# Four moves in the first head of a hybrid mLSTM and HGRN2 step: gate exponentials, decay exponentials, weight loads, a convolution

## The chip, the core and the metric

The kernel runs on one core of one Trainium2 chip. The metric is the device time of one execution in microseconds (us). Engines are called as the profile calls them: PE is TensorE's matmuls, PEld its weight loads, ACT is ScalarE, DVE is VectorE, POOL is GpSimd, SP is SyncE, which here only issues DMAs. "L1042" is line 1042 of the kernel before.

## The reference, cut to what matters

One inference step of a one-layer streaming encoder. 512 prompt frames of a new stream and 32 frames of a running stream go through it together, so the kernel's row length T is 544. Two branches work on the same normalised input: an mLSTM with 4 heads of width 512 and an HGRN2 with 8 heads of width 128. The change is all within the mLSTM's first head.

```python
xn = _rmsnorm(h, norm_g[l])
proj = xn @ w_in[l]
u, v_m, z_m, ig_pre, fg_pre, q_h, f_h, i_h, g_h, ga, gb = jnp.split(proj, ...)
c, conv_new = _causal_conv(u, conv0[l], conv_w[l], conv_b[l])   # 4 taps
c = jax.nn.silu(c)
qm, km = c @ w_qm, (c @ w_km) * M_HD ** -0.5        # per head
lf = jax.nn.log_sigmoid(fg_pre + b_fg[l])
# _mlstm, per head, chunk by chunk:
dmat = jnp.exp(logd - m_t[..., None])               # decay between positions
s = (q @ k^T) * dmat
num = w_inter * (C @ q) + s @ v                     # C: memory from before
C_new = decay * C + (w_last * v)^T @ k
...
hm = _head_layernorm(hm, mnorm_g[l])
hm = (hm + m_skip[l] * c) * jax.nn.silu(z_m)
ya = hm @ w_brm[l]                                  # mLSTM's branch output
```

The HGRN2 branch (`yb`), the sigmoid merge of `ya` and `yb`, `w_out`, the per-layer embedding and a final norm follow. Everything is float32.

## The kernel before, in words

**Precision.** A float32 product is made of three fp32r products. Each operand is split into a high part, which ACT makes as a rounded copy, and a low part, which DVE makes by subtraction: `split` does it for activations (L105, L106) and `split_piece` for pieces of weights (L132, L133). A name with `h` or `l` at its end is one of these parts, and one with `r` in it is the raw piece that a DMA loaded. A matmul group on low parts cannot start before ACT and then DVE are done.

**Tiling.** Weights come as pieces of 128 rows by 512 columns through a ring of buffers. An output tile has 128 rows and is made as two halves of 272 columns in PSUM. `phalves` gives these from four banks, and `paux` gives one of two double banks to everything else (scores `sc`, transposes `kt`, `kts` and `yt`, the old memory's product `nm`).

**Order.** PE runs one list of matmuls in a fixed order (`tc.manual_schedule` holds PE's order as written). On ACT, DVE, POOL and SP a scheduler sets the order, from the order in which the code issues the instructions, from `tc.high_priority()`, and from `tc.issue_after(x)`, which holds an instruction back in that order until x. Each engine then runs its list strictly in order, so one that waits holds up everything behind it. Between the steps of a head a `Pump` gives PE blocks of projection (`d`, from `fill(h)`: this head's `z`, the next head's `u`, the merge gates), so that PE has work while ACT and DVE make the next operands.

**Head 0, in time order.** (1) The head's values `vp` (L1397) are made from eight weight pieces `wv0` to `wv7`, k = 0 to 7, four banks at a time, with ACT and DVE scaling and splitting the input at the same time (`norm` L1287 and L1290, `norm_low` L1294; the tiles are `x`, `xh`, `xl`). Among them `stage_gates` makes the forget gates' log-sigmoid on a 4-row tile (`row`): an Exp and a Ln (L727, L728), each with a load of ACT's table. `vq` (L1407) is the running stream's value product, `vhl`, `vh` and `vl` are the values out of PSUM (`value_out`, L1317 and L1318), and the first blocks of `d` (L387: `z`, on weights `wi32`) follow on the banks that these release. (2) `stage_k`, `stage_q` make keys and queries; `qf` (L857) and `q` (L860, L861) are the copies of the queries out of PSUM. (3) `stage_decay` loads the row maxima to all partitions (`bc`), and ACT makes the decay tiles `dm` with ten exponentials and one small one (L810, L811). `hgrn_bounds` adds one small exponential (`lbe`). A dummy silu (L866) then loads the silu table. (4) `stage_scores` (L881) multiplies queries by keys, and DVE multiplies by the decay (L889). (5) `mchain`: keys are transposed (`kt`) and weighted (`kwh`, `kwl`), old memory `c` is loaded in four pieces (L986), and `nm` (L1042) multiplies it by the decayed queries `qw`; then new memory (`C`), scores by values (`nm` L1096), the layer norm, and the transposes `yt` (L1144). DVE adds the skip path (L1151, L1152, in `c0` to `c3`), multiplies by `silu(z)` (L1153), and `split` makes `hm0` to `hm3`. (6) `stage_br` multiplies these by `w_brm` (pieces `wbm`) to `ya` (L167), and ACT copies it out (L1171).

The next head's causal convolution is made tile by tile in `conv`: one scaling on ACT (L646), three DVE multiply-adds (L651, `cv`), a silu on ACT (L657, L658), and a split to `cs4` and so on (the names go on over the heads: `cs4` to `cs7` are head 1's). Its first tile is called from `inner` (in `fill`), when the `u` tile is out of PSUM, and the others from `stage_br` after each of its `u` steps.

Of the kernel before, what the change touches and what calls it, by code (L numbers as in the profile page):

```python
# [9 lines left out]
F32 = mybir.dt.float32  # L10
# [3 lines left out]
AF = mybir.ActivationFunctionType  # L14
# [8 lines left out]
T = NS + NP  # L23
# [43 lines left out]
def hybrid_step(ctx: ExitStack, tc: tile.TileContext, a, o):  # L67
# [34 lines left out]

    def split(src, name):
        hi, lo = slot(name + "h", F32R), slot(name + "l", F32R)
        S.copy(hi[:, :T], src)  # L105
        V.tensor_tensor(lo[:, :T], src, hi[:, :T].bitcast(F32), ALU.subtract)  # L106
        return hi, lo

    def pair_tile(name, ring):
# [562 lines left out]
    def fill(h):  # L672


        def value(f, t):
            st8[h]["vt"][f] = t

        def gate(f, t):
            act = S.activation(t[:, :T], t[:, :T], AF.Silu)
            st8[h]["z"][f] = (t, act)  # L680

        def gate_one(f, acc):
            z = eslot(f"z{h}{f}")
            for b in range(2):
                with tc.high_priority():
                    if f < 2:
                        out = V.tensor_tensor(z[:, half(b)], acc[b][:, :TH], rb[:, half(b)], ALU.mult)
                    else:
                        out = V.tensor_copy(z[:, half(b)], acc[b][:, :TH])
            st8[h].setdefault("copies", []).append(out)  # L690
            act = S.activation(z[:, :T], z[:, :T], AF.Silu)
            st8[h]["z"][f] = (z, act)

        def inner_tile(f):
            ub = conv_tile((h + 1) * KH + f)
            return ub, conv_parts(ub)

        def inner(f, ub):
            st8[h + 1]["ub"][f] = ub
            if f == 0:  # L700
                conv(h + 1)

        st8[h]["z"] = [None] * KH
        todo = []
        if h:
            st8[h]["vt"] = [None] * KH
            todo += [pair("v", f, 16 + h * KH + f, lambda f: plain(eslot(f"vt{h}{f}")), value) for f in (0, 2)]
            todo += [pair("z", f, 32 + h * KH + f, lambda f: plain(eslot(f"z{h}{f}")), gate) for f in (0, 2)]
        else:
            todo += [One(("z", f), 32 + f, TH, lambda acc, f=f: gate_one(f, acc), x0 if f < 2 else None) for f in range(KH)]  # L710
        if h + 1 < MH:
            st8[h + 1]["ub"] = [None] * KH
            todo += [pair("u", f, (h + 1) * KH + f, inner_tile, inner) for f in (0, 2)]
            todo[-1].urgent = True
        return todo
# [76 lines left out]
                combo[(b, b + i)] = len(combo)  # L792
        return col, cols, combo

    def stage_decay(h):

        bc = tp.tile([P, T + NS], F32, tag="bc", name=f"bc{h}")
        nc.sync.dma_start(bc, nm_d[h : h + 1, :].to_broadcast([P, T + NS]))
        d01 = [slot(f"dm{h}0"), slot(f"dm{h}1")]
        d2 = slot(f"dm{h}2")  # L800
        dj = [d01[0][:, 0:512], d01[1][:, 0:384], d2[:, 0:256], d2[:, 256:384]]
# [4 lines left out]
        for j in range(NB):  # L806
            for i in range(j, NB):
                d = dj[j][:, (i - j) * P : (i - j + 1) * P]
                src = d if i == j else bc[:, NS + i * P : NS + (i + 1) * P]
                S.activation(d, src, AF.Exp, bias=col[:, combo[(j, i)], h : h + 1])  # L810
# [35 lines left out]
    def stage_q(h, u):  # L846
# [6 lines left out]
        for f in range(2):  # L853
# [6 lines left out]
                    read = S.copy(qh[:, half(b)], acc[b])  # L860
                    low = V.tensor_tensor(ql[:, half(b)], acc[b], qh[:, half(b)].bitcast(F32), ALU.subtract)  # L861
            t["qs"].append((qh, ql))
        if u:

            with tc.issue_after(read.ins):
                S.activation(small("silu", [1, 2]), ident[:1, :2], AF.Silu)  # L866
        return low

    def stage_scores(h):
# [86 lines left out]
    def mchain(h, pump):  # L956
# [26 lines left out]
            low = V.scalar_tensor_tensor(kws[lo], pt[lo, 0, :], wc[lo], kws[lo].bitcast(F32), ALU.mult, ALU.subtract)  # L983
        c0 = [eslot(f"c0{h}{f}") for f in range(KH)]
        for f in range(KH):
            nc.sync.dma_start(c0[f][:, :VW], a["C0"][h, f])  # L986

        if h == 0:
            vv, vs = t["vv"], t["vs"]
# [146 lines left out]
        for f in range(KH):  # L1136
# [13 lines left out]
            with tc.high_priority():  # L1150
                V.scalar_tensor_tensor(c[:, NS:T], pt[:, 0, :], g, c[:, NS:T], ALU.mult, ALU.add)  # L1151
                V.scalar_tensor_tensor(c[:, :NS], pt[:, 1, :NS], g, c[:, :NS], ALU.mult, ALU.add)  # L1152
            V.tensor_tensor(c[:, :T], c[:, :T], z[:, :T], ALU.mult)  # L1153
            hs.append(split(c[:, :T], f"hm{ft}"))
# [62 lines left out]
    with tc.manual_schedule(engines={mybir.EngineType.Activation, mybir.EngineType.DVE, mybir.EngineType.PE}):  # L1217
# [147 lines left out]
        for k in range(KD):  # L1365
            if k == 1:
# [71 lines left out]
    with tc.manual_schedule(engines={mybir.EngineType.PE}):  # L1438
        for h in range(MH):
# [14 lines left out]
            if h == 0:  # L1454
# [561 lines left out]
```

## Time and profile before

| what | value |
|---|---|
| time, median of 3 runs | 1132.48 us (1131.96 to 1132.76) |
| the profiled execution's own time | 1132.39 us |
| its span in the trace | 1130.5 us |
| its granted PE clock, mean | 0.998 |
| PE busy | 1112.0 us, 98% of the span |
| DVE, ACT and POOL busy | 79%, 59% and 15% |
| HBM traffic over the span | 138 GB/s |

The span is the time from the trace's first to its last instruction; 1.9 us of the execution lie around it. PE is idle for some 18 us in all, and that is where the table must be read with care: a busy share of 98% over the whole program says nothing on the stretch in which head 0 runs. Most of PE's waits are there.

### The profile page before, as it was taken

Reading aid. Unit: us, or ns where it says so; the run is one execution under the profiler, and the core shown is the slowest. Engines: PE = TensorE matmul, PEld = TensorE weight load, DVE = VectorE, ACT = ScalarE, POOL = GpSimd, SP = SyncE. Lnnn points to the kernel's source line nnn. Section 1 sums busy time; section 2 is a strip of 40 time slices with the busy share of each in tenths; the row PEclk is TensorE's granted clock in tenths of the full one; section 3 lists DMA queues with packets and bytes.
Section 4 is the critical chain, followed back from the end, with each engine's and each line's share of the span. In section 5 each row is a group of like instructions: output and inputs, shape, how many; then the busy total and the mean of one; then the engine's idle time right before and its main releaser. Section 6 shows DMA issues by size and latency. Waiting matters only on the chain.

```text
span 1130.5 us, 23774 instructions
## 1 busy us (share of the span) xinstructions
PE 1112.0 (98%) x8733; PEld 1087.1 (96%) x8733; DVE 895.3 (79%) x2040; ACT 670.6 (59%) x1506; POOL 169.2 (15%) x308
## 2 busy tenths in 40 slices
PE   9999998999999999999999999999999999999998
PEld 9879898999999999999999999999999999999998
DVE  6888878578697695986888799999999977654485
ACT  6677356655566463765556467776776667333462
POOL 7223000000020000200100122322332210000000
PEclk9999999999999999999999999999999999999999
DMA  6133323513344232553667666666765685332753
GB/s 229 55 112 108 103 85 96 161 54 123 128 154 165 63 115 104 163 167 96 188 188 223 196 140 147 136 144 147 157 140 148 158 220 161 117 102 72 260 152 117
DMA packets 90139, 157.94 MB, mean 140 GB/s; under 512 B 10148, under 2 KB 17828, under 8 KB 90024
## 3 DMA queue, kind: packets, MB, share of 16 engines
q1 hardware_dynamic: 80352, 139.33, 39.0%
q0 software_dynamic: 8784, 15.99, 9.1%
q8 instruction: 68, 1.11, 0.4%
q10 hardware_dynamic: 888, 1.12, 0.3%
q14 instruction: 47, 0.39, 0.1%
HBM read 131.49 MB, written 24.91 MB: 138 GB/s over the span
## 4 chain that ended last, share of the span: by engine, by line
PE 90%; DVE 5%; DMA 2%; ACT 2%; issue 1%; SPq 0%; POOL 0%; ACTq 0%; DVEq 0%
PE d L502 37%; PE ya L167 8%; PE pg L1863 4%; PE yb L167 4%; PE o L167 4%; PE q L167 4%; PE C L921 4%; PE k L167 4%; PE nm L1096 3%; PE sc L881 3%; PE pl L1635 2%; PE u L287 2%; PE vp L1397 1%; PE ple L167 1%; PE d L387 1%
## 5 line engine op out<-in xcount | busy, mean ns | idle before, releaser
L420 POOL DMA_DIRECT2D ws<-in_w_in x46 | 40.4, 884 | 237.6 <-DVE hkq L1659 49.5
L516 ACT COPY t<-d 128x272 f32<-128x272 f32 x126 | 47.7, 378 | 8.8 <-PE d L502 8.7
L1659 DVE TENSOR_TENSOR hkq<-hkq,q 128x288 f32<-128x288 f32 (+1 forms) x96 | 40.7, 430 | 3.3 <-ACT t L516 1.2
L1635 PE MATMUL pl<-hkq,km 128*128 128x128 f32 x224 | 37.8, 291 | 1.2 <-ACT km L1624 1.1
L651 DVE SCALAR_TENSOR_TENSOR cv<-ub,vec,cv 128x547 f32<-128x547 f32 x48 | 37.6, 782 | 0.4
L1635 PEld LDWEIGHTS pl<-hkq,km 128*128 128x128 f32 x224 | 31.2, 189 | 2.7 <-ACT km L1624 2.3
L1624 ACT COPY km<-hkq 128x256 f32<-128x256 f32 x56 | 24.0, 428 | 14.0 <-DVE hkq L1659 4.6
L1030 DVE SCALAR_TENSOR_TENSOR c<-c,wi,Cs 128x258 f32<-128x258 f32 x32 | 15.3, 479 | 18.5 <-PE Cs L1028 18.2
L933 ACT COPY Co<-C 128x258 f32<-128x258 f32 x30 | 9.8, 378 | 30.6 <-PE C L921 28.3
L1174 DVE TENSOR_TENSOR y<-ya,y 128x272 f32<-128x272 f32 x48 | 18.8, 434 | 8.8 <-PE ya L167 8.7
L1666 DVE COPY_PREDICATED at<-lmask,pl 128x256 f32<-128x256 uint8 (+1 forms) x56 | 25.2, 450 | 0.1
L1107 ACT COPY y<-nm 128x516 f32<-128x516 f32 x16 | 9.5, 591 | 22.7 <-PE nm L1096 22.4
L643 POOL COPY uo<-ub 128x3 f32<-128x3 f32 x16 | 17.5, 1092 | 34.9 <-DVE ub L525 27.5
L1603 POOL TENSOR_SCALAR_AFFINE_SELECT aa<-at 128x128 f32<-128x128 f32 x32 | 19.6, 643 | 8.2 <-DVE at L1666 8.0
L821 POOL COPY vsm<-vt 128x96 f32<-128x96 f32 x12 | 7.3, 607 | 87.7 <-DVE vt L523 45.3
L1084 DVE BATCH_NORM_STATS2 bs<-y 128x6 f32<-128x512 f32 (+1 forms) x20 | 13.8, 689 | 8.0 <-ACT y L1107 7.8
L477 POOL DMA_DIRECT2D ws<-in_w_in x15 | 15.6, 1037 | 28.3 <-DVE ws272l L133 23.6
L1096 PE MATMUL nm<-vhl,sh 128*128 128x258 f32 x112 | 18.4, 286 | 0.6 <-ACT y L1107 0.6
L895 ACT CAST sh<-dm 128x512 fp32r<-128x512 f32 (+3 forms) x16 | 7.4, 460 | 17.7 <-DVE dm L889 17.7
L1850 DVE TENSOR_TENSOR h<-o,h 128x272 f32<-128x272 f32 x16 | 6.3, 436 | 14.5 <-PE o L167 14.5
L1765 ACT ACTIVATE osq<-kq 128x128 f32<-128x128 f32 x32 | 9.8, 305 | 12.3 <-DVE kq L1760 12.1
L1837 DVE TENSOR_TENSOR gb<-yb,gb 128x272 f32<-128x272 f32 x16 | 6.3, 435 | 13.1 <-PE yb L167 13.1
(4496 smaller groups left out, 4998.4 us busy)
## 6 DMA issues: line engine op xcount, KB each, us to landing
ws<-in_w_in POOLq DMA_DIRECT2D x61, 256.0 KB, 4.9
ws<-in_w_in SPq DMA_DIRECT2D x46, 256.0 KB, 3.9
ya_d<-y SPq DMA_DIRECT2D x32, 272.0 KB, 2.2
y<-ya_d SPq DMA_DIRECT2D x24, 272.0 KB, 4.1
c<-in_C SPq DMA_DIRECT2D x16, 258.0 KB, 3.8
out_Cs<-c SPq DMA_DIRECT2D x16, 258.0 KB, 2.9
out_Cp<-Co SPq DMA_DIRECT2D x12, 258.0 KB, 2.7
x<-in_xT SPq DMA_DIRECT2D x8, 272.5 KB, 4.9
```

What stands on the lines that cost most here:

```text
L167: PE.matmul(both[b][:m, :TH], part(w, off + k * step, m, x), xx[:, half(b)], start=(k == 0 and j == 0), stop=(k == n - 1 and j == 2),)
L420: G.dma_start(t, w_in[u][:, i * WP : (i + 1) * WP], accum_op=ALU.add)
L502: PE.matmul(ps, ww[:, c], xx, start=(start and k == 0 and j == 0), stop=end, skip_group_check=not start,)
L516: self.kept = S.copy(t, ps)
L651: V.scalar_tensor_tensor(cv[:, :547], ub[:, j : j + 547], vcol(V_CW + 4 * ft + j), cv[:, :547], ALU.mult, ALU.add)
L881: PE.matmul(pn[:, 0, :n], ks[f][x][:, j * P : (j + 1) * P], qs[f][y][:, NS + j * P : T], start=(f == 0 and i == 0), stop=(f == KH - 1 and ...
L921: PE.matmul(pn[g][:, :VH], kw[b][x][:, f * P : (f + 1) * P], vv[b][y][:, g * VH : (g + 1) * VH], start=(b == 0 and j == 0), stop=(b == NB ...
L1096: PE.matmul(pn[:, g, :VH], st[j][x][:, (i - j) * P : (i - j + 1) * P], vv[j][y][:, g * VH : (g + 1) * VH], start=(j == 0 and q == 0), stop ...
L1635: PE.matmul(pn[:, 0, b * P : (b + 1) * P], km[:, b * P : (b + 1) * P], view(qq, b * P, ((2 * c, P // (2 * c)), (HB + c, 2), (1, c))), star ...
L1659: V.tensor_tensor(x, x, d, ALU.mult)
L1666: V.copy_predicated(at[:, :n], lmask[:, li, :n], pn[:, 0, :n])
L1863: PE.matmul(ps, part(w, k * P, P, x), xx[:, c], start=(k == 0 and j == 0), stop=(k == KD - 1 and j == 2))
```

## The change

It has four parts, all in head 0 or at its end.

1. **Rows' exponentials among the values.** At k == 1, before the input's `norm(0)`, the code issues one more `value_weight()` (`wv6`) and `next(gates)`, the step of `stage_gates` with Exp and Ln. Before, both stood two norms further on, at k == 2.
2. **Decay behind the last query.** The load of `bc` becomes a function `decay_rows`. For head 0 it is issued where `stage_decay` stood, and `stage_decay` follows after `stage_q(h, 1)`, with its exponentials held back until the last copy of the queries. The dummy silu comes after them, held until the last decay.
3. **Branch weights' loads behind old memory's.** In `stage_br` of head 0 the pieces for u = 0 and 1 are held back until the last load of old memory.
4. **Next convolution later.** Head 1's first convolution tile is no longer called from `inner` but at the start of `stage_br`, held back until `hm3`'s high part. The product with `silu(z)` and the splits to `hm` have high priority in head 0.

```diff
     def split(src, name):
...
+        made[name] = S.copy(hi[:, :T], src), V.tensor_tensor(lo[:, :T], src, hi[:, :T].bitcast(F32), ALU.subtract)
...
         def inner(f, ub):
             st8[h + 1]["ub"][f] = ub
-            if f == 0:
+            if f == 0 and h:
                 conv(h + 1)
...
+    def decay_rows(h):
         bc = tp.tile([P, T + NS], F32, tag="bc", name=f"bc{h}")
         nc.sync.dma_start(bc, nm_d[h : h + 1, :].to_broadcast([P, T + NS]))
+        return bc
+
+    def stage_decay(h, bc=None, after=None):
+        bc = bc or decay_rows(h)
...
+                with tc.issue_after(after.ins) if after is not None else nullcontext():
+                    S.activation(d, src, AF.Exp, bias=col[:, combo[(j, i)], h : h + 1])
...
-        if u:
+        if u and h:
             with tc.issue_after(read.ins):
                 S.activation(small("silu", [1, 2]), ident[:1, :2], AF.Silu)
+        t["read"] = read
...
-            nc.sync.dma_start(c0[f][:, :VW], a["C0"][h, f])
+            t["c0"] = nc.sync.dma_start(c0[f][:, :VW], a["C0"][h, f])
...
+            with nullcontext() if h else tc.high_priority():
+                V.tensor_tensor(c[:, :T], c[:, :T], z[:, :T], ALU.mult)
+                hs.append(split(c[:, :T], f"hm{ft}"))
...
     def stage_br(h, after=None):
         hs = st8[h]["hs"]
+        if h == 0:
+            with tc.issue_after(made["hm3"][0].ins):
+                conv(1)
         for u in range(4):
-            with tc.issue_after(after.ins) if after is not None and u == 0 else nullcontext():
+            first = after if u == 0 else None
+            if h == 0 and u < 2:
+                first = st8[0]["c0"]
+            with tc.issue_after(first.ins) if first is not None else nullcontext():
                 w = weight(a["w_brm"][h, u], f"wbm{h}{u}")
...
                 gates = stage_gates(fg, ig)
                 next(gates)
                 value_weight()
+                value_weight()
+                next(gates)
                 silu_low(3)
                 norm(0)
...
                 norm(2)
-                next(gates)
-                value_weight()
                 norm(3)
...
-                stage_decay(h)
-                lower_bounds = hgrn_bounds(st8[0]["decayed"])
+                bc0 = decay_rows(h)
...
             low = stage_q(h, 1)
             if h == 0:
+                stage_decay(h, bc0, st8[0]["read"])
+                lower_bounds = hgrn_bounds(st8[0]["decayed"])
+                with tc.issue_after(st8[0]["decayed"].ins):
+                    S.activation(small("silu", [1, 2]), ident[:1, :2], AF.Silu)
```

PE's list of matmuls is the same in both kernels. Three places show what moved on the other engines. The line numbers are each kernel's own (up to L697 a number is one less in the kernel after).

First ACT during the values. Before, from the split of weight piece 5 on (`wv5h`); the two `L727` and `L728` pairs are Exp and Ln on the gates' rows:

```order
L132 CAST wv5h_684<-wv5r_682 128x512
L1290 CAST xh0_690<-x0_79 128x544
L1290 CAST xh1_694<-x1_83 128x544
L132 CAST wv6h_711<-wv6r_709 128x512
L1290 CAST xh2_718<-x2_87 128x544
L727 ACT_TABLE_LOAD
L727 ACTIVATE row0_721<-row0_721 4x544
L728 ACT_TABLE_LOAD
L728 ACTIVATE row0_721<-row0_721 4x544
L132 CAST wv7h_727<-wv7r_725 128x512
```

And after:

```order
L131 CAST wv5h_684<-wv5r_682 128x512
L131 CAST wv6h_690<-wv6r_688 128x512
L726 ACT_TABLE_LOAD
L726 ACTIVATE row0_694<-row0_694 4x544
L727 ACT_TABLE_LOAD
L727 ACTIVATE row0_694<-row0_694 4x544
L1303 CAST xh0_700<-x0_79 128x544
L1303 CAST xh1_704<-x1_83 128x544
L131 CAST wv7h_721<-wv7r_719 128x512
L1303 CAST xh2_728<-x2_87 128x544
```

The exponentials and `wv6h` moved ahead of the input's splits, and `wv7h` now has two of these behind it instead of the exponentials ahead of it.

Second SP's queue around old memory's loads (`c000` to `c003`, from `in_C0`), where `bc2` is the next head's row load. Before:

```order
L798 DMA bc2_4854<-nm_d_1223 128x576
L122 DMA wbm00r0_2418<-in_w_brm 128x512
L986 DMA c000_1675<-in_C0 128x516
L986 DMA c001_1676<-in_C0 128x516
L986 DMA c002_1677<-in_C0 128x516
L986 DMA c003_1678<-in_C0 128x516
L122 DMA wbm00r512_2420<-in_w_brm 128x512
L122 DMA wbm01r0_2504<-in_w_brm 128x512
```

And after:

```order
L797 DMA bc2_4854<-nm_d_1223 128x576
L992 DMA c000_1675<-in_C0 128x516
L992 DMA c001_1676<-in_C0 128x516
L992 DMA c002_1677<-in_C0 128x516
L992 DMA c003_1678<-in_C0 128x516
L121 DMA wbm00r0_2418<-in_w_brm 128x512
L121 DMA wbm00r512_2420<-in_w_brm 128x512
L121 DMA wbm01r0_2504<-in_w_brm 128x512
```

The first branch weight's load moved from ahead of the four to behind them.

Third DVE at the end of head 0, from the first skip addition on (`c0_570` to `c3_669` are the four tiles; `hm0l` is the first low part for the branch product). Before:

```order
L1151 SCALAR_TENSOR_TENSOR c0_570<-yt0_2255,vec_78,c0_570 128x512
L1152 SCALAR_TENSOR_TENSOR c0_570<-yt0_2255,vec_78,c0_570 128x32
L1151 SCALAR_TENSOR_TENSOR c1_629<-yt1_2279,vec_78,c1_629 128x512
L523 TENSOR_TENSOR ub4_2093<-d41_2092,t164_2149 128x272
L1152 SCALAR_TENSOR_TENSOR c1_629<-yt1_2279,vec_78,c1_629 128x32
L1151 SCALAR_TENSOR_TENSOR c2_662<-yt2_2314,vec_78,c2_662 128x512
L133 TENSOR_TENSOR ws46l_2361<-ws26_2169,ws46h_2360 128x512
L1151 SCALAR_TENSOR_TENSOR c3_669<-yt3_2338,vec_78,c3_669 128x512
```

And after:

```order
L1157 SCALAR_TENSOR_TENSOR c0_570<-yt0_2255,vec_78,c0_570 128x512
L1158 SCALAR_TENSOR_TENSOR c0_570<-yt0_2255,vec_78,c0_570 128x32
L1157 SCALAR_TENSOR_TENSOR c1_629<-yt1_2279,vec_78,c1_629 128x512
L1160 TENSOR_TENSOR c0_570<-c0_570,z00_978 128x544
L522 TENSOR_TENSOR ub4_2093<-d41_2092,t164_2149 128x272
L1157 SCALAR_TENSOR_TENSOR c2_662<-yt2_2300,vec_78,c2_662 128x512
L1158 SCALAR_TENSOR_TENSOR c1_629<-yt1_2279,vec_78,c1_629 128x32
L1158 SCALAR_TENSOR_TENSOR c2_662<-yt2_2300,vec_78,c2_662 128x32
```

The first tile's product with `silu(z)` moved in behind the second tile's large addition, and that tile's small addition moved behind the third's large one.

Last ACT in the same stretch, where `cv4`, `c4` and `cs4h` are head 1's first convolution tile. Before:

```order
L105 CAST hm1h_2289<-c1_629 128x544
L132 CAST wbm011h_2512<-wbm01r512_2506 128x512
L527 ACTIVATE ub7_2199<-d60_2194 128x32
L527 ACTIVATE ub7_2199<-d60_2194 128x240
L646 ACTIVATE cv4_2302<-ub4_2093,vec_78 128x547
L132 CAST wbm020h_2594<-wbm02r0_2590 128x512
L657 ACTIVATE c4_2307<-cv4_2302 128x32
L658 ACTIVATE c4_2307<-cv4_2302 128x512
L105 CAST cs4h_2310<-c4_2307 128x544
L105 CAST hm2h_2324<-c2_662 128x544
L105 CAST hm3h_2348<-c3_669 128x544
```

And after:

```order
L105 CAST hm1h_2289<-c1_629 128x544
L105 CAST hm2h_2310<-c2_662 128x544
L131 CAST wbm010h_2508<-wbm01r0_2504 128x512
L105 CAST hm3h_2334<-c3_669 128x544
L131 CAST wbm011h_2512<-wbm01r512_2506 128x512
L526 ACTIVATE ub7_2199<-d60_2194 128x32
L526 ACTIVATE ub7_2199<-d60_2194 128x240
L645 ACTIVATE cv4_2406<-ub4_2093,vec_78 128x547
L131 CAST wbm020h_2594<-wbm02r0_2590 128x512
```

`hm2h` and `hm3h` moved ahead of the convolution's silu and split, and its first step `cv4` now follows `hm3h`.

More of the change, by code (lines that the diff above doesn't have):

```diff
@@ L104, in split @@
         hi, lo = slot(name + "h", F32R), slot(name + "l", F32R)
-        S.copy(hi[:, :T], src)
-        V.tensor_tensor(lo[:, :T], src, hi[:, :T].bitcast(F32), ALU.subtract)
+        made[name] = S.copy(hi[:, :T], src), V.tensor_tensor(lo[:, :T], src, hi[:, :T].bitcast(F32), ALU.subtract)
         return hi, lo
@@ L793, in stage_cols @@
         return col, cols, combo
-    def stage_decay(h):
+    def decay_rows(h):
         bc = tp.tile([P, T + NS], F32, tag="bc", name=f"bc{h}")
         nc.sync.dma_start(bc, nm_d[h : h + 1, :].to_broadcast([P, T + NS]))
+        return bc
+    def stage_decay(h, bc=None, after=None):
+        bc = bc or decay_rows(h)
         d01 = [slot(f"dm{h}0"), slot(f"dm{h}1")]
@@ L809, in stage_decay @@
                 src = d if i == j else bc[:, NS + i * P : NS + (i + 1) * P]
-                S.activation(d, src, AF.Exp, bias=col[:, combo[(j, i)], h : h + 1])
+                with tc.issue_after(after.ins) if after is not None else nullcontext():
+                    S.activation(d, src, AF.Exp, bias=col[:, combo[(j, i)], h : h + 1])
         decayed = S.activation(ds, ds, AF.Exp, bias=cols[:, 0, h : h + 1])
@@ L1152, in mchain @@
                 V.scalar_tensor_tensor(c[:, :NS], pt[:, 1, :NS], g, c[:, :NS], ALU.mult, ALU.add)
-            V.tensor_tensor(c[:, :T], c[:, :T], z[:, :T], ALU.mult)
-            hs.append(split(c[:, :T], f"hm{ft}"))
+            with nullcontext() if h else tc.high_priority():
+                V.tensor_tensor(c[:, :T], c[:, :T], z[:, :T], ALU.mult)
+                hs.append(split(c[:, :T], f"hm{ft}"))
         t["hs"] = hs
```

## The prediction

> **What bounds the kernel now.** I read three views: the page's busy times, PE's waits, and the timeline of each engine at the places that the waits name.
>
> ```profile
> PE 1112.0 (98%) x8733; PEld 1087.1 (96%) x8733; DVE 895.3 (79%) x2040; ACT 670.6 (59%) x1506; POOL 169.2 (15%) x308
> ```
>
> ```profile
> PE ya L167 <- ACT hm2h L105: 4.6, 1, 4.6
> PE vp L1397 <- ACT wv7h L132: 1.5, 1, 1.5
> PE d L387 <- DVE vhl L1318: 1.3, 2, 1.1
> PE nm L1042 <- DMA c<-in_C: 1.2, 1, 1.2
> ```
>
> ```profile
> 70.00:100.00 30.00, 29.93 (x246) 29.46 (x245) 28.99 (x61) 24.91 (x52) 16.23 (x15) 1.00 0.34 105
> ...
> 185.00:210.00 25.00, 25.00 (x192) 25.00 (x192) 16.25 (x35) 18.87 (x47) 0.00 (x0) 0.95 0.44 142
> ```
>
> ```profile
> 177.00:188.00 11.00, 6.05 (x35) 5.62 (x34) 9.47 (x15) 5.50 (x12) 1.08 (x2) 0.84 0.43 121
> ```
>
> PE bounds: it is busy for 98%, and its list is the same after the change, so time can come only out of its waits, or out of stretches in which it runs slowly. The second view gives in each row the total, the number and the longest of a wait: these four, its longest, are 8.6 us, and the change touches what ends each. The windows give width, then busy time of PE, PEld, DVE, ACT and POOL, PE's granted clock, DMA share and GB/s. A wait's row is only the idle part. How much later PE gets through a place I take from starts: the actual start of a later matmul less the start that it would have had at the usual spacing.
>
> **Part 1, rows' exponentials among the values.** PE's and ACT's timeline (start, duration, and in brackets the idle time before and what ended it):
>
> ```profile
> 56.85 0.63 PE L1397 MATMUL vp<-wv6h,x 128*128 128x512 f32 x2
> ...
> 57.55 0.63 PE L1397 MATMUL vp<-wv6h,x 128*128 128x512 f32 x2
> ...
> 59.89 0.73 PE L1397 MATMUL vp<-wv7h,x 128*128 128x512 f32 x2 [1.47 <-ACT wv7h L132]
> ...
> 63.58 0.59 PE L1407 MATMUL vq<-wv4r,xg 128*32 128x512 f32 x1
> ...
> 66.38 0.42 PE L387 MATMUL d<-x,wi320l 128*128 128x272 f32 x2
> 66.63 0.54 PE L387 MATMUL d<-x,wi320h 128*128 128x272 f32 x3
> ```
>
> ```profile
> 47.46 0.60 ACT L132 CAST wv5h<-wv5r 128x512 fp32r<-128x512 f32 x1
> ...
> 55.41 1.28 ACT L727 ACT_TABLE_LOAD   x1
> ...
> 59.23 0.60 ACT L132 CAST wv7h<-wv7r 128x512 fp32r<-128x512 f32 x1
> ...
> 62.88 1.25 ACT L1317 ACTIVATE vhl<-vp,rms_r 128x512 fp32r<-128x512 f32 x2
> ```
>
> Groups follow each other every 57.55 - 56.85 = 0.70, so `wv7` was due at 58.25 and began at 59.89: 1.64 lost. The split came late since two table loads and two functions, 59.23 - 55.41 = 3.82 in all, stood ahead of it. In the new order the chain from 48.06 is `wv6h` 0.6, the same 3.8, two input splits at 0.6: `wv7h` starts near 53.9 and ends near 54.5. The exponentials read a row that DVE makes first; with 3.8 us to spare a late row does no harm.
>
> A second loss hangs on the first. The `d` blocks need the four value banks back. `vq`'s last group starts at 63.58 and takes about 0.46, so `d` was due near 64.04 and its third pair, at 0.25 a pair (66.38 to 66.63), near 64.54; it started at 66.38: 1.8 lost. ACT's copies out of PSUM began only at 62.88, because the splits of `wi32` stood ahead of them, late for the same reason. Now these can be done before the banks end, and the copies start as each bank ends (59.3 on); two copies of 0.63 and two subtractions of about as much are over at about 62.0, and the need is 64.04 - 1.64 = 62.4. So the second loss goes too: **gain 3.4**. Bounds: 1.6 if the second loss stays, 3.4 if both go; I take the upper, to which the 0.4 of slack is nearer. The input splits are now later by some 2 us; the blocks up to 66.63 read `x`, not `xh`, so nothing on PE waits for them.
>
> **Part 2, decay behind the last query.**
>
> ```profile
> 106.94 0.63 PE L881 MATMUL sc<-q,kh 128*128 128x512 f32 x2
> ...
> 108.60 0.98 PE L881 MATMUL sc<-q,kh 128*128 128x512 f32 x2 [0.81 <-ACT q L860]
> ...
> 109.64 0.51 PE L881 MATMUL sc<-q,kh 128*128 128x384 f32 x2
> ```
>
> ```profile
> 104.56 0.38 ACT L860 CAST q<-q 128x272 fp32r<-128x272 f32 x1
> ...
> 108.16 0.38 ACT L860 CAST q<-q 128x272 fp32r<-128x272 f32 x1
> ```
>
> The last group of the first score was due one group (0.70, as for the values) after 106.94, at 107.64, the next score at 108.34; that began at 109.64: **1.3 lost**. Between the queries' two halves, which begin 108.16 - 104.56 = 3.6 apart, ACT made all the exponentials; some 3.3 are theirs. Without them the second half is copied at about 104.9 to 105.3, and DVE's subtraction ends near 105.7, two us early. The exponentials then run from 105.3 to 108.6; the first four are over at 106.5, and DVE first multiplies by them when the first score ends, near 108.6. The silu table follows (1.28 as in part 1), to about 109.9, so the first scores' split on ACT may be half a microsecond late. What hides that is that PE reads these splits only in `nm` L1096, after the transposes and old memory. `bc` of head 2, queued on SP behind these exponentials, moves by half a microsecond, and nothing needs it here. POOL's copy of `wi` reads the same load as before. Gain 1.3; the lower bound is the 0.8 of idle.
>
> **Part 3, branch weights' loads behind old memory's.**
>
> ```profile
> 119.69 0.66 PE L966 MATMUL kt<-ident,kf 128*128 128x128 f32 x4
> ...
> 124.13 0.41 PE L387 MATMUL d<-xh,wi350l 128*128 128x272 f32 x2
> 125.76 2.65 PE L1042 MATMUL nm<-c,qw 128*32 128x258 f32 x8 [1.21 <-DMA c<-in_C]
> ...
> 128.58 0.64 PE L1042 MATMUL nm<-c,qw 128*32 128x258 f32 x8
> ```
>
> ```profile
> 121.90 1.85 SPq L986 DMA_DIRECT2D c<-in_C  x4
> ```
>
> ```profile
> c<-in_C SPq DMA_DIRECT2D x16, 258.0 KB, 3.8
> ...
> x<-in_xT SPq DMA_DIRECT2D x8, 272.5 KB, 4.9
> ```
>
> The first `nm` group was due at 124.13 + 0.25 = 124.38 and the second began at 128.58; the second's eight matmuls took 0.64, and with the small one behind them 0.7 pass. So 4.2 - 0.7 = 3.5 are lost, three times the 1.2 of idle, because the eight matmuls then waited for one piece after the other. SP issued the four loads from 121.90 on, about 0.46 apart, after the branch weight ahead of them had its buffer. Without that, the first piece's buffer is free long before, and the three others wait for the last key transposes (from 119.69 on; which waits a load has is read from the new program): issues at about 120.0, 120.5 and 120.9. At the median 3.8 they land at 123.8, 124.3 and 124.7. PE needs the last of them a little after 124.4, so 0 to 0.3 are left: **gain 3.3**. Bounds: with a landing of 4.9, the slowest median on SP's queue, the last piece comes at 125.8 and 1.2 are left, a gain of 2.3; the upper end is 3.5. The branch weights, now behind the four, still lie some 50 us ahead of the branch product (178.64, below).
>
> **Part 4, next convolution later.**
>
> ```profile
> 178.64 0.41 PE L167 MATMUL ya<-hm1h,wbm000l 128*128 128x272 f32 x2
> 183.66 0.52 PE L167 MATMUL ya<-hm2h,wbm001h 128*128 128x272 f32 x2 [4.61 <-ACT hm2h L105]
> ...
> 185.13 0.65 PE L167 MATMUL ya<-hm2h,wbm001l 128*128 128x272 f32 x2
> ...
> 187.80 0.41 PE L167 MATMUL ya<-hm0h,wbm000l 128*128 128x272 f32 x2
> ```
>
> ```profile
> 181.64 0.23 ACT L657 ACTIVATE c<-cv 128x32 f32<-128x32 f32 x1 [3.42 <-DVE cv L651]
> ```
>
> From 178.64 to 187.80 there are nine pairs; at 0.25 they take 2.26 and end at 180.90. So 6.9 are lost: 4.6 idle, and most of the other 2.3 because pairs came every 0.45 until 187.80 (six in the 2.67 from 185.13). The `hm2` split stood on ACT behind head 1's convolution, whose silu waited 3.42 for DVE. In the new order the splits need no convolution: counted through the new lists of ACT and DVE with the durations of the same instructions before, `hm2l` is done at about 177.5 and `hm3l` at 178.7, and PE needs `hm2` no sooner than 178.9.
>
> The slow pairs show a lower clock: the window from 177 to 188 has 0.84, the one from 185 to 210 has 0.95. They begin where the wait ends, so I count the 2.3 with it. Behind the wait of 1.47 in part 1 no such spacing shows. The Trainium skill ("TensorE: Matmul & The Clock Gate", Part 1: The HAM clock gate) has a rule for this: an idle window of about 3.4 us halves the clock, and as long a busy stretch brings it back. The trace agrees with it here, with 4.61 of wait and then some 4 us of slow pairs; by it the sum is the one below.
>
> Were the slow pairs due to something else than the wait, 4.6 would be gained and the sum would be 2.3 smaller.
>
> The new order has a price on DVE:
>
> ```profile
> 169.47 0.75 DVE L1151 SCALAR_TENSOR_TENSOR c<-yt,vec,c 128x512 f32<-128x512 f32 x1
> ...
> 172.28 1.99 DVE L1153 TENSOR_TENSOR c<-c,z 128x544 f32<-128x544 f32 x3
> ```
>
> ```profile
> 170.02 0.60 PE L1144 MATMUL yt<-ident,y 128*128 128x128 f32 x4
> ```
>
> The fourth transpose, at 170.02, needs the double bank that the second tile's small addition releases. That addition ended just before 169.5; now it stands behind a product (1.99 / 3 = 0.65) and the third tile's large addition (0.75, of which some 0.1 overlaps with the next), 1.3 later, near 170.85. PE waits some **0.85**; the bounds are 0 and 1.3. Net gain 6.9 - 0.85 = 6.05.
>
> The convolution that was done early now lies after 185, with one tile more to make there: on DVE about 3.1 (three multiply-adds at 0.8 and a subtraction at 0.7) of the 25.00 - 16.25 = 8.75 that DVE is free from 185 to 210. Counted through the same lists, the last tile's low part is done about 2 us before head 1's keys read it.
>
> **The sum.** 3.4 + 1.3 + 3.3 + 6.05 = 14.05, from the profiled execution's 1132.39 (span 1130.5): 1118.3, or 1118.4 against the median of 1132.48, which is 0.09 above. About 0.2%, 2.3 us, is what a measurement of this kernel can tell from no change.
>
> **The rivals.** *The gain of part 1 is given back* (0.14). DVE is busy for 28.99 of the 30 us from 70 to 100; if PE then waited for it, all 3.4 would go: 1121.8. For it speaks that row. Against it: DVE's work there begins behind PE's first `z`,
>
> ```profile
> 71.98 0.79 DVE L687 TENSOR_TENSOR z<-d,rb 128x272 f32<-128x272 f32 x2 [0.79 <-PE d L387]
> ```
>
> for which it waited 0.79, so its work starts earlier with PE.
>
> *Old memory still lands late* (0.12): at 4.9 a load, 1.2 stay, 1119.4, or 1.0 above my sum. For it speaks that the four share the queue, against it the median of 3.8.
>
> *Part 4 gives only the idle time* (0.08): 1118.4 + 2.3 = 1120.7. Against it speaks that the slow pairs begin with the wait's end and stop 4 us later.
>
> *The convolution comes too late* (0.03), the side on which the kernel is slower. Head 1's keys need all four tiles; if ACT's copies of `ya` and the convolution's steps hold each other up, PE waits in front of `k`. It decides where that wait passes the sum of 14 plus 2.3: the last tile would have to come 2 + 16 us later than I reckon, 1135 and above. The 8.75 of spare DVE time against 3.1 speak against it.
>
> *Something in between* (0.03): a wait of 12 to 16 us that I don't see, which leaves no change. That the change does not do what it says is ruled out by the order, where all four moves are seen.
>
> **How the numbers follow.** My forecast, 1117.5 to 1119.3 by itself (the 0.85 between 0 and 1.3, and 0.5 on part 2), has 0.60; with it stand 0.14, 0.12, 0.08, 0.03 and 0.03. Faster holds the first four, 0.94; same 0.03; slower 0.03. The range goes from 1116.2, which is the sum without the 0.85 and with about as much from waits that I count as left, to 1122.8, where part 1 gives nothing and old memory is 1.0 late.
>
> **What would show it.** PE's waits without rows for `wv7h`, `vhl` before `d`, `q` before `sc` and `hm2h` before `ya`; `nm` L1042's first group under 1.0 long instead of 2.65; a new wait of `yt` for DVE near 0.85; the clock near 1.00 where the branch product runs. I am wrong where a wait of PE before head 1's `k`, or before `d` between 70 and 100, gives the time back.

## The result, and the profile after

| kernel | median | from to | ratio to before (95% interval) |
|---|---|---|---|
| before | 1132.76 us | 1131.96 to 1134.16, 5 runs | |
| after | 1122.35 us | 1119.90 to 1123.12, 5 runs | 0.9902 (0.9887 to 0.9917) |

The change is worth 10.4 us, against 14 forecast. The time lies inside the stated range, at its upper end, and outside the 1117.5 to 1119.3 of the forecast by itself. The profiled execution of the kernel after took 1120.93 us, 1.4 less than the median, with a span of 1119.0.

The page's busy times and PE's waits of the kernel after (total, number, longest):

```profile
PE 1108.0 (99%) x8733; PEld 1085.5 (97%) x8733; DVE 896.4 (80%) x2040; ACT 669.9 (60%) x1506; POOL 167.8 (15%) x308
```

```profile
PE k L166 <- DVE z L686: 1.1, 1, 1.1
PE d L501 <- DVE ub L522: 0.8, 1, 0.8
PE yt L1150 <- DVE c L1158: 0.8, 1, 0.8
...
PE k L166 <- ACT kf L839: 0.5, 1, 0.5
```

All the waits that the change aimed at are gone, and four new ones have come, each behind DVE or ACT: `z` is the `z` block's scaling out of PSUM, `kf` the keys' copy out of PSUM, `ub` the next head's `u` tile out of PSUM, and `c` the skip addition. The same PE instructions, in the same order, stand in both traces, so their starts can be set against each other. A negative number says how much earlier the kernel after is at that place:

| PE instruction | before | after | difference | step since the row above |
|---|---|---|---|---|
| last `vp` group of `wv6l` | 57.32 | 57.02 | -0.30 | from the first 12 us, not the change |
| third `z` pair | 66.38 | 62.50 | -3.88 | -3.58, part 1 |
| a `k` pair of the last key tile | 87.72 | 85.84 | -1.88 | **+2.00**, the two new waits before `k` |
| second score's first matmul | 109.64 | 106.45 | -3.19 | -1.31, part 2 |
| second `nm` group | 128.58 | 122.30 | -6.28 | -3.09, part 3 |
| `d` on `ws16h` | 172.86 | 168.55 | -4.31 | **+1.97**, the new waits of `yt` and `d` |
| a pair of `ya` | 187.80 | 176.70 | -11.10 | -6.79, part 4 |
| span | 1130.5 | 1119.0 | -11.5 | |

Three places of the timeline answer to those of before: `wv7` is in its place, the first `nm` group takes 0.75 instead of 2.65, and the pairs of `ya` follow every 0.25.

```profile
57.95 0.63 PE L1410 MATMUL vp<-wv7h,x 128*128 128x512 f32 x2
...
121.39 0.75 PE L1048 MATMUL nm<-c,qw 128*32 128x258 f32 x8
...
174.45 0.41 PE L166 MATMUL ya<-hm1h,wbm000l 128*128 128x272 f32 x2
174.70 0.41 PE L166 MATMUL ya<-hm2h,wbm001h 128*128 128x272 f32 x2
```

**Where 2.0 us before `k` went.** Behind the first of the two waits PE is 2.28 earlier than before, so that wait took 1.60 of the 3.88. At the second, for `kf`, PE loses 0.89, where the kernel before lost 0.49 at the same place; that is the other 0.40. For the first wait, DVE, POOL and PE of the kernel after:

```profile
70.04 1.81 DVE L732 SCALAR_TENSOR_TENSOR row<-fg,row 4x544 f32<-4x544 f32 x1
71.88 0.69 DVE L1436 TENSOR_TENSOR vsum<-vq,vsum 32x512 f32<-32x512 f32 x1
72.50 2.42 DVE L736 TENSOR_TENSOR_SCAN row<-rst,row 4x544 f32<-4x544 f32 x1
...
76.20 0.77 DVE L737 SCALAR_TENSOR_TENSOR row<-ig,vec,row 4x544 f32<-4x544 f32 x1
...
77.86 0.79 DVE L686 TENSOR_TENSOR z<-d,rb 128x272 f32<-128x272 f32 x2
```

```profile
70.00 1.28 POOL L132 TENSOR_TENSOR wk010l<-wk01r,wk010h 128x512 fp32r<-128x512 f32 x1 [0.24 <-ACT wk010h L131]
72.47 1.30 POOL L132 TENSOR_TENSOR wk011l<-wk01r,wk011h 128x512 fp32r<-128x512 f32 x1 [1.20 <-ACT wk011h L131]
```

```profile
78.35 0.74 PE L166 MATMUL k<-cs0h,wk000h 128*128 128x272 f32 x2 [1.11 <-DVE z L686]
```

And the same two DVE instructions and one POOL subtraction in the kernel before:

```profile
73.41 0.77 DVE L733 SCALAR_TENSOR_TENSOR row<-fg,row 4x544 f32<-4x544 f32 x1
...
74.83 1.65 DVE L737 TENSOR_TENSOR_SCAN row<-rst,row 4x544 f32<-4x544 f32 x1
```

```profile
73.57 1.77 POOL L133 TENSOR_TENSOR wk010l<-wk01r,wk010h 128x512 fp32r<-128x512 f32 x1
```

The gate row took 0.77 before and 1.81 after, the scan 1.65 and 2.42. After, POOL's subtraction begins 0.04 and 0.03 us ahead of DVE's instruction, and DVE is the one that takes long; before, DVE begins 0.16 ahead, and POOL's subtraction takes 1.77 instead of 1.28. The second `z`, which PE waits for, stands behind both on DVE. After, POOL's subtraction ends at 71.28 and the row 0.57 later; POOL's next one ends at 73.77 and the scan 1.15 later. With POOL idle the two take 0.70 and 1.27 (e1, below), so all but some 0.13 of each came when POOL was done. The scan of before is between the two: it began while POOL's subtraction had 0.5 to go. The Trainium skill tells of this ("SBUF — State Buffer", Who interferes with whom): a DVE instruction with two inputs in SBUF and a GpSimd instruction that reads SBUF contend, the second to issue blocks, and the order of issue decides which. Both traces agree, but for those 0.13.

**The second place.** The fourth transposes wait for DVE's small addition, as forecast, and a block `d` then waits for `ub`, a wait that was not forecast. DVE and PE after:

```profile
163.70 0.74 DVE L1157 SCALAR_TENSOR_TENSOR c<-yt,vec,c 128x512 f32<-128x512 f32 x1
164.36 0.40 DVE L1158 SCALAR_TENSOR_TENSOR c<-yt,vec,c 128x32 f32<-128x32 f32 x2
164.68 1.35 DVE L1160 TENSOR_TENSOR c<-c,z 128x544 f32<-128x544 f32 x2
...
167.46 0.72 DVE L1160 TENSOR_TENSOR c<-c,z 128x544 f32<-128x544 f32 x1
168.10 0.40 DVE L522 TENSOR_TENSOR ub<-d,t 128x240 f32<-128x240 f32 x1
```

```profile
164.75 0.63 PE L1150 MATMUL yt<-ident,y 128*128 128x128 f32 x4 [0.78 <-DVE c L1158]
...
168.55 0.40 PE L501 MATMUL d<-xfh,ws16h 128*128 128x272 f32 x1 [0.78 <-DVE ub L522]
```

The addition that makes `ub`, and so releases `d`'s bank, now stands behind the products of all four tiles, three of which are seen here (1.35 and 0.72). Before, all four came behind it, from 172.28 on.

### The profile page after: what moved, and what is told of

It reads as the page before. It is cut to its first block, busy times and chain, and to the rows that moved or that the text cites. A ratio compares the mean times of both kernels' runs of the same rounds, so it can differ in the third digit from the quotient of the medians.

```text
span 1119.0 us, 23773 instructions
## 1 busy us (share of the span) xinstructions
PE 1108.0 (99%) x8733; PEld 1085.5 (97%) x8733; DVE 896.4 (80%) x2040; ACT 669.9 (60%) x1506; POOL 167.8 (15%) x308
## 3 DMA queue, kind: packets, MB, share of 16 engines
q8 instruction: 68, 1.11, 0.4%
## 4 chain that ended last, share of the span: by engine, by line
PE 92%; DVE 4%; DMA 1%; ACT 1%; issue 1%; SPq 0%; POOL 0%; ACTq 0%; POOLq 0%; DVEq 0%
PE d L501 36%; PE ya L166 9%; PE pg L1879 4%; PE yb L166 4%; PE q L166 4%; PE o L166 4%; PE C L927 4%; PE k L166 4%; PE sc L887 3%; PE nm L1102 3%; PE pl L1651 2%; PE u L286 2%; PE vp L1410 2%; PE ple L166 1%; PE d L386 1%; DMA ws<-in_w_in 1%
## 5 line engine op out<-in xcount | busy, mean ns | idle before, releaser
L1102 PEld LDWEIGHTS nm<-vhl,sh 128*128 128x128 f32 x112 | 15.4, 190 | 1.2 <-ACT y L1113 0.8
```

The source lines that it names most:

```text
L1102: PE.matmul(pn[:, g, :VH], st[j][x][:, (i - j) * P : (i - j + 1) * P], vv[j][y][:, g * VH : (g + 1) * VH], start=(j == 0 and q == 0), stop ...
```

## The experiments

Ratios are to the kernel before in runs of the same chip. "Earlier" means against the start of the same PE instruction in the kernel before, as in the table. The runs come from several chips, on which the kernel before has medians from 1132.31 to 1133.43, so two variants' times can differ by about 1 us for the chip alone.

**e1: the low halves of wk01 on DVE.**

```diff
-        st8[0]["wk1"] = weight(a["w_km"][0, 1], "wk01", eng=G)
+        st8[0]["wk1"] = weight(a["w_km"][0, 1], "wk01")
```

> The changed kernel, but the low halves of the second key weight (wk01) are made on DVE instead of POOL, so that POOL runs nothing beside DVE's gate row and scan. In the changed kernel these two took 1.81 and 2.42 us against 0.77 and 1.65 before, each begun 0.03 to 0.04 us behind a POOL subtraction, and PE then waited 1.11 us before k for the second z. Theory 1 (POOL holds DVE up through SBUF): row and scan take 0.8 and 1.65 again, the second z starts near 76.2 instead of 77.86 although DVE has 1.2 us more to do, and the wait before k is under 0.3; total about 1.0 to 1.5 us below the changed kernel's. Rival (DVE is simply full there): row and scan stay long or the 1.2 us come on top; the second z starts at 78 or later and the wait grows to about 1.7; total 0.6 us above the changed kernel's.

1118.38 us (1118.11 to 1119.27), ratio 0.9875 (0.9860 to 0.9890). DVE in its trace:

```profile
70.10 0.70 DVE L732 SCALAR_TENSOR_TENSOR row<-fg,row 4x544 f32<-4x544 f32 x1
...
71.45 1.27 DVE L736 TENSOR_TENSOR_SCAN row<-rst,row 4x544 f32<-4x544 f32 x1
...
76.08 0.79 DVE L686 TENSOR_TENSOR z<-d,rb 128x272 f32<-128x272 f32 x2
...
78.18 0.77 DVE L737 SCALAR_TENSOR_TENSOR row<-ig,vec,row 4x544 f32<-4x544 f32 x1
```

Row and scan are short, the second `z` comes 1.8 us earlier although DVE has more to do, and no wait before `k` is left. The rival, that DVE is simply full, falls. At the key row of the table PE is 4.45 earlier instead of 1.88, 2.6 us more, where 1.0 to 1.5 were expected.

Not all of this is the collision, because the edit also changed the scheduler's order. DVE's next gate row (L737), ahead of the second `z` in the kernel after, now stands behind it, which is 0.77 of the 1.8. With it ahead, `z` would begin near 76.85, and `k`, which began 0.49 behind it in the kernel after, near 77.34, an estimate: some 0.35 late, not 1.27. And ACT's second pair of `kf` copies now stands ahead of the gate row's table load. First the kernel after, then e1:

```profile
82.17 1.28 ACT L755 ACT_TABLE_LOAD   x1
...
84.90 0.66 ACT L839 ACTIVATE kf<-k 128x272 f32<-128x272 f32 x2
```

```profile
80.79 0.69 ACT L839 ACTIVATE kf<-k 128x272 f32<-128x272 f32 x2
81.50 1.28 ACT L755 ACT_TABLE_LOAD   x1
```

So of the 2.6, 1.6 are the wait for `z` and 0.9 the wait for `kf`. At the second `nm` group only 1.75 is left: the loads of old memory were issued as far ahead as in the kernel after, but the last landed 4.4 us behind its issue instead of 3.6, and the first `nm` group took 1.65 instead of 0.75.

```profile
119.79 0.59 PE L1048 MATMUL nm<-c,qw 128*32 128x258 f32 x2 [0.43 <-DMA c<-in_C]
```

The medians of e1 and the kernel after differ by 4.0 and the spans of their traces by 2.6. Most of what head 0 does not explain in the spans comes between 560 and 800 us, where the traces of e1 to e7 and e9 to e11 drift apart by up to 1.7 us from the kernel after and from each other.

**e2: gate rows held until the second z.**

```diff
-                with tc.issue_after(st8[0]["copies"][0].ins):
+                with tc.issue_after(st8[0]["copies"][1].ins):
                     next(gates)
```

> The changed kernel, with the gates' row, scan and what follows them held until the second z's copy instead of the first's. Theory 1 and the rival both say that the second z then comes before PE needs it, so the wait of 1.11 before k goes; what is open is whether the gate rows, which now come some 5 us later, hold up something behind: the row maxima's load, the decay or the queries. If nothing does, PE is about 3.5 us earlier at the scores than in the kernel before its own first-query loss, instead of 1.87, and the total is 1.6 to 2.0 below the changed kernel's; if the rows are late, a new wait of PE among the queries takes part of it or more.

1120.86 us (1119.29 to 1121.23), ratio 0.9893 (0.9877 to 0.9909). The wait before `k` is gone, as both theories expected, and PE is 4.34 earlier there; but the late gate rows cost a new wait at the first query:

```profile
87.70 0.67 PE L166 MATMUL q<-cs0h,wq000h 128*128 128x272 f32 x2 [1.39 <-ACT kf L839]
```

The collision can be avoided by moving DVE's side too, but that side has less slack than POOL's.

**e3: high priority for the hm splits alone.**

```diff
-            with nullcontext() if h else tc.high_priority():
-                V.tensor_tensor(c[:, :T], c[:, :T], z[:, :T], ALU.mult)
+            V.tensor_tensor(c[:, :T], c[:, :T], z[:, :T], ALU.mult)
+            with nullcontext() if h else tc.high_priority():
                 hs.append(split(c[:, :T], f"hm{ft}"))
```

> The changed kernel, but only the splits to hm have high priority in head 0, not the product with silu(z) ahead of them. In the changed kernel PE waits 0.78 for the fourth transposes (the small addition stands behind a product) and 0.78 for a u tile's copy (behind the product of the fourth tile). Theory: both waits come from the product's priority; without it both go, hm2 and hm3 are still there in time, and the total is 1.6 to 1.9 below the changed kernel's. Rival: the products are then late, the branch product waits for hm, and the gain is under 0.5 or a loss.

1119.99 us, from 1117.26 to 1122.69: too wide to settle 1.8 us, ratio 0.9896 (0.9874 to 0.9918). The trace settles it: neither the wait of `yt` nor that of `ub` is left, `hm` is in time, and between the second `nm` group and the pair of `ya` at 187.80 PE gains 6.5, where the kernel after gained 4.8.

**e4: e2 and e3 together.**

> The edits of the two runs before together: gate rows behind the second z, and high priority for the hm splits alone. If both theories hold and the two places don't touch, the total is 3.2 to 3.9 below the changed kernel's, about 1118.7; if either fails, the sum of what the two gave alone.

1117.93 us (1117.61 to 1119.00), ratio 0.9871 (0.9856 to 0.9886), with e2's wait at the first query still there, 1.4. It is 4.4 below the kernel after, where 3.2 to 3.9 were expected.

**e5: e1 and e3 together.**

> The changed kernel with two edits: the low halves of wk01 on DVE, and high priority for the hm splits alone. The first alone gave 1118.4 with little spread, the second removed two waits of PE of 1.9 us together. If the two places are independent: about 1116.5, and a spread under 1.5 us, since the collision of POOL and DVE that can go either way is gone. If they are not: 1118 or more.

1117.45 us (1116.90 to 1118.04), ratio 0.9855 (0.9842 to 0.9869), the fastest of all: 4.9 below the kernel after. It is 1 us above what was expected, and its trace shows one reason, another way in which the second `z` can be late without POOL: the first key weight landed late, ACT waited for it, and the copy of `vsum`, behind it on ACT, held DVE up.

```profile
68.11 0.62 ACT L131 CAST wk000h<-wk00r 128x512 fp32r<-128x512 f32 x1 [1.78 <-DMA wk00r<-in_w_km]
69.58 0.62 ACT L131 CAST wk001h<-wk00r 128x512 fp32r<-128x512 f32 x1 [0.85 <-DMA wk00r<-in_w_km]
```

```profile
78.34 0.74 PE L166 MATMUL k<-cs0h,wk000h 128*128 128x272 f32 x2 [0.64 <-DVE z L686]
```

**e6, e7, e9, e10: one part undone each, on top of e1.** e1's edit stays in, so that the collision doesn't blur what is compared. In e6 `value_weight()` and `next(gates)` stand behind `norm(2)` again; in e7 `conv(h + 1)` is back in `inner`, with no high priority; in e9 `stage_decay`, `hgrn_bounds` and the dummy silu are where they were; in e10 these two lines are out:

```diff
-            if h == 0 and u < 2:
-                first = st8[0]["c0"]
```

> The changed kernel with wk01's low halves on DVE (1118.4), with part 1 undone: the exponentials again behind the input's splits. Theory: part 1 is worth its whole 3.4 to 3.6 once the collision is gone, so 1121.8 to 1122.0. Rival (DVE is full from 70 to 100 and gives the gain back in any case): 1119 to 1120.

> The changed kernel with wk01's low halves on DVE (1118.4), with part 4 undone: the convolution again from inner, and no high priority. The trace of the changed kernel has part 4 at 6.8 gained and two new waits of PE with 1.9 in all: 1118.4 + 4.9 = 1123.3. My prediction had 6.05 net: 1124.4. If part 4's gain is partly given back later in the program: below 1122.5.

> The changed kernel with wk01's low halves on DVE (1118.4), with part 2 undone: decay and its row load ahead of the last query again. Theory: 1.3 is lost again before the scores, 1119.7. If the price of the silu table behind the decay was paid elsewhere, less: 1118.4 to 1119.2.

> The changed kernel with wk01's low halves on DVE (1118.4), with part 3 undone: the branch weights' first load ahead of old memory's again. Theory: the wait before nm returns with its eight matmuls that wait for one piece after the other, 3.1 to 3.5 lost: 1121.5 to 1121.9. If only the wait of 1.2 counts: 1119.6.

| without | median | ratio (95% interval) | over e1's 1118.38 | what is back in the trace |
|---|---|---|---|---|
| part 1 | 1121.53 | 0.9894 (0.9880 to 0.9908) | 3.2 | the wait for `wv7h`, 1.47 |
| part 2 | 1121.14 | 0.9897 (0.9874 to 0.9919) | 2.8 | a wait of `sc` for `q`, 0.47 |
| part 3 | 1121.80 | 0.9897 (0.9875 to 0.9920) | 3.4 | two waits of `nm` for `c`, 1.6 |
| part 4 | 1125.60 | 0.9927 (0.9914 to 0.9941) | 7.2 | the wait of `ya`, 4.6, and slow pairs |

In each of the four, every run is slower than e1's slowest (1119.27), but by the intervals of the ratios only part 4 is clear of e1; the traces say how much goes where. Part 1 is worth nearly its whole sum, once POOL is out of DVE's way: PE is 3.8 later at the last key tile than in e1. With part 3 undone, PE loses 2.5 at the first `nm` group against e1, which itself loses 0.9 there, so 3.4 in all: what the eight matmuls lost and not just the wait. Part 2's runs go from 1119.88 to 1123.43, so the 2.8 say little; in the trace 1.2 is lost there.

Part 4 is dearer by time (7.2) than by its trace, where PE is 5.3 later behind `ya` than in e1. That is more than the 4.9 expected, since the slow pairs lasted 5.8 us here, from 175.3 to 181.2, against 4.1 in the kernel before, behind a wait of the same 4.61. The two spans differ by 6.7; most of the other 1.4 come between 560 and 800 us, for a reason that stays open.

**e8: the wait filled, in the kernel before.** 36 matmuls whose results are not used, ahead of the first that reads `hm2h`:

```diff
         for k, (xh, xl) in enumerate(xs):
+            if name == "ya000" and k == 2:
+                spare = paux("spare")
+                for _ in range(36):
+                    PE.matmul(spare[:m, 0, :TH], part(w, off, m, 0), xs[0][0][:, half(0)], start=True, stop=True)
```

> The kernel before, with 36 more matmuls of 128x272 into a spare bank where PE waits 4.6 us for hm2h, on operands that are ready; their results are not used. They take 36 x 0.125 = 4.5 us and fit in the wait. If the slow pairs behind the wait come from PE's having been idle, they are fast now: the pairs behind hm2h come every 0.25 instead of 0.45, the clock in that window is near 1.00, and the total is 1.8 to 2.3 below the kernel before's. If they come from something else: the pairs stay at 0.45 and the total is that of the kernel before, or 0.3 above it.

```profile
179.48 4.68 PE L168 MATMUL spare<-hm0h,wbm000h 128*128 128x272 f32 x36
...
185.47 0.41 PE L171 MATMUL ya<-hm2h,wbm001l 128*128 128x272 f32 x2
185.72 0.42 PE L171 MATMUL ya<-hm3h,wbm001h 128*128 128x272 f32 x2
```

```profile
177.00:188.00 11.00, 10.58 (x83) 10.14 (x82) 10.04 (x16) 5.79 (x14) 1.31 (x2) 1.00 0.40 121
```

The pairs come every 0.25 and the clock is 1.00 where it was 0.84. From 0.58 late at 169 PE gets to 0.82 early at 187: 1.4 gained there. So the slow pairs do come from PE's idling. Of the 2.3 that the prediction counted beyond the idle 4.6 they are 1.4; about 0.7 stay, behind the short wait for `hm2l`, which e8 has as well (0.33 idle). The total, expected 1.8 to 2.3 below the kernel before, did not follow: 1134.88 us (1130.48 to 1136.99), ratio 1.0009 (0.9997 to 1.0022). In the trace PE loses 4.6 again between 600 and 960 us, among it eight waits for `km` where the kernel before has two:

```profile
PE pl L1639 <- ACT km L1628: 3.5, 8, 1.4
```

Whether the filling has to do with that, or whether it is the spread of that stretch from run to run, is not settled.

**e11: the kernel after, a second trace.**

> The changed kernel itself once more, nothing edited, for a second trace. In the run with e3's edit, which leaves this place alone, the gate row began 0.2 us ahead of POOL's subtraction and took 0.82, and PE's wait before k was 0.21 instead of 1.11. Theory: which of the two engines begins first is chance, by when the key weight's load lands, so a second trace of the same program can show the row either at 0.8 (POOL's subtraction then at 1.8) or at 1.8 (POOL's at 1.3), never both long or both short while they overlap; the wait before k goes with it, 0 to 0.4 or 0.9 to 1.3. Rival: the same durations as in the first trace, to a tenth, with the cause in the program's order.

1121.67 us (1120.52 to 1124.21), ratio 0.9912 (0.9885 to 0.9939).

```profile
70.96 0.83 DVE L732 SCALAR_TENSOR_TENSOR row<-fg,row 4x544 f32<-4x544 f32 x1
...
72.44 1.66 DVE L736 TENSOR_TENSOR_SCAN row<-rst,row 4x544 f32<-4x544 f32 x1
```

```profile
71.19 1.77 POOL L132 TENSOR_TENSOR wk010l<-wk01r,wk010h 128x512 fp32r<-128x512 f32 x1
...
73.40 1.79 POOL L132 TENSOR_TENSOR wk011l<-wk01r,wk011h 128x512 fp32r<-128x512 f32 x1 [0.44 <-ACT wk011h L131]
```

```profile
77.85 0.74 PE L166 MATMUL k<-cs0h,wk000h 128*128 128x272 f32 x2 [0.28 <-DVE z L686]
```

The same program, and now DVE begins 0.2 and 1.0 ahead, and POOL is the long one. The row is short; the scan, begun while POOL's first subtraction had 0.5 to go, took 1.66, as before the change. The wait before `k` is 0.28 instead of 1.11. So the collision can go either way from one execution to the next.

What differs ahead of it is how the two halves of the key weight landed: 1.2 us apart in the first trace of the kernel after, 0.7 apart here, in e3's trace and in the kernel before. With 1.2, POOL was through with its earlier subtraction and began as soon as ACT's split was there, just ahead of DVE's row; with 0.7 it was still busy. Four traces fit this; no run tests it by itself.

From the third `z` pair to the last key tile PE loses 1.16 here instead of 2.00, and the difference is that of the two waits for `z`. The rest is not the collision alone: both halves landed later here, so that DVE's row began 0.92 later, and the wait for `kf` is there again (0.48).

## Why the prediction was right, and where a size was off

The four gains came where and nearly as large as they were forecast. The total came out right in part by luck: the range's upper end, 1122.8, was meant for part 1 giving nothing and old memory 1.0 late. What came instead was 2.0 lost behind part 1 and 1.1 more than counted behind part 4, and the median is 0.45 below that end.

- **Part 1.** 3.4 was forecast, 3.58 came, at the place and by both losses that were named. The step that failed stands behind it: the rival that this gain is given back, put at 0.14, came true by 2.0 of 3.4. I had argued against it that DVE's work starts earlier with PE. The first `z` did (3.88 earlier). The gate rows behind it did not, as POOL's subtractions, moved by another amount, now met them the other way round, and as the key weight's landing moved along only in part (ACT's first split of it began 3.6 earlier in the first trace, 2.2 in the second). I read DVE's 28.99 of 30 us as work; some 0.8 of it was waiting for POOL even then (row 0.77 against 0.70, scan 1.65 against 1.27, a subtraction `xl` 1.02 against 0.70), which a busy time doesn't show. 1.6 of the 2.0 are the wait behind these on DVE, 0.4 the `kf` copy on ACT.
- **Part 2.** 1.3 forecast, 1.31 in the trace. The silu table ended at 108.2, and the first scores' split followed at once; nothing on PE waited.
- **Part 3.** 3.3 forecast, 3.09 in the trace, 3.4 when undone in e10. The first `nm` group took 0.75, so the loads were in time but for about 0.1. The last of them landed at 121.40, with that group begun at 121.39, so there is next to no slack: in e1 the rival of the late landing came true by 0.9. The 4.9 taken for it as the slowest median on SP's queue is the slowest only among the page's rows; the full list of the kernel before has 5.5 and more for other transfers.
- **Part 4.** 6.9 forecast, 6.79 in the trace. The slow pairs went with the wait, and e8 shows in another way that they belong to it. The price on DVE was right for the fourth transposes (0.78 of wait, 0.85 forecast), but as large a wait follows 4 us later for the same reason, and that one I had not followed to the instructions behind on DVE. e3 removes both.
- **The convolution's lateness** didn't happen: no wait before head 1's `k`.
- **The sum.** 14.05 was forecast; 3.58 - 2.00 + 1.31 + 3.09 - 1.97 + 6.79 = 10.80, and 0.3 from the start make the 11.1 of the table. So the two steps marked there, 2.0 and the 1.1 of 1.97 that was not counted, are the 3 us between forecast and trace. The medians miss by 3.95, 0.7 more; that the first trace is of one of the faster runs is part of it. With both places mended, e5 takes 1117.45 against 1118.4 forecast. That agrees, though it is no exact proof: e5 also lacks the 0.85 that the forecast counted, and has a late `z` again for another reason.

## What to carry to other kernels

Where stalls are removed one after the other, the lists of the engines that now run closer together must be followed to the next wait of PE, and past it: both steps that were missed lay mainly on DVE, one a few instructions behind the place that was worked out. Two engines that hold each other up, as DVE and POOL here, make a collision whose side can flip with a shift of 0.2 us. A change far ahead of it can cost or save 0.8 us there, and one trace of before does not tell which. An edit that takes one engine out of it also reorders the other lists, so what it gains is to be taken apart place by place. The same instruction's duration in two traces (0.77 and 1.81) is the sign to look for.

## What the runs showed of the hardware that was not expected

- DVE's 4x544 row instruction took 0.70 with POOL idle, 0.77 to 0.83 when it began ahead of POOL's subtraction, and 1.81 when it began 0.04 behind it; POOL's 128x512 subtraction took 1.28 when first and 1.77 when second. The scan took 1.27 with POOL idle, 1.65 when it began with 0.5 us of a POOL subtraction to go, and 2.42 when it began 0.03 behind one.
- Filling a wait of 4.6 us with matmuls that do nothing kept PE's pairs at 0.25 (0.45 without), at the same start of the pair behind the wait to within 0.02, the kernel's own shift of 0.58 taken off. It brought 1.4 us at the place and nothing measurable in the total.
- Behind a wait of PE of 4.61 in both, the slow pairs lasted 4.1 us in the kernel before and 5.8 in e7.
